# State products of the first eleven heads written to the two score tiles of PSUM, instead of the two rotating tiles

## The chip, the cores and the metric

The kernel runs on one core of one Trainium2 chip. The metric is the device time of one execution in microseconds (us), lower is better; the times shown are medians of several executions. Five engines work side by side: TensorE (PE in the profile; its loads of the stationary operand are listed apart as PEld), VectorE (DVE), ScalarE (ACT), GpSimd (POOL) and SyncE (SP). Matmul results go to PSUM tiles, and DVE and ACT read them there.

## The reference, cut to what matters

One layer of a decoder trunk over 1024 tokens of width 1024. One input projection feeds two mixers, HGRN2 (8 heads, key and value width 128) and GLA (4 heads, key width 128, value width 256). Both are gated linear attention, per head:

```
S_t = diag(a_t) S_{t-1} + k_t v_t^T
o_t = S_t^T (scale * q_t)
```

It can be computed in chunks: with the decays folded into q and k, the output of a chunk is (scores inside the chunk) times v, plus q times the state S left by the chunks before; and each chunk adds its own product k^T v to the state, which is decayed first. Each branch is then normalised, gated and projected, the branches are merged by sigmoid gates, projected again, added to x and normalised.

## The kernel before, in words

Everything is held with channels on the 128 partitions. Large projections are split into a rounded part and a remainder (two fp32r factors, three matmuls for one); they take most of TensorE's time: L607 (`mm_feat`, one 128-channel feature over 1024 tokens, 8 x 6 matmuls of 128x512), L2000 (the value and HGRN stages) and L1422/L1599 (gates, branches, output).

The twelve heads are a side track. `attention` (L639) is a Python generator that is advanced from the main stream of projections (`Stream.weave`): after each unit of projection matmuls the next piece of the running head is issued. Heads run one after the other, the four GLA heads first, then the eight HGRN2 heads; `me` counts them from 1. A tile scheduler then orders the instructions of each engine by priority and by its own costs, and puts in the semaphore waits; so the order on an engine is not quite that of the source. It knows which tile each instruction reads and writes: a write to a tile waits for the earlier readers of the same tile.

A head has 8 chunks of 128 tokens. Its pieces, in order:

- Scores: small matmuls (L665, L698, L756, L762, L767) into the two fixed PSUM tiles `sc_ps[0]` and `sc_ps[1]`. DVE (L676 to L681, L735 to L743, L771) and ACT (L776, L779) read them into `blk` and `scT`.
- Transposes of k (L791) into two tiles from `mtile()`, copied by ACT to `kT` (L792).
- State products (L815): k^T v of chunks 0 to 6 into a PSUM tile `pu`, four chunks to a tile in an HGRN2 head (two tiles), two to a tile in a GLA head (four tiles). DVE takes them into the states one after the other: a copy for the first (L819) and six steps `state(ch+1) = state(ch)*decay + product` (L821). This is called the state chain here. Its seven results are states 1 to 7.
- Outputs: for each half of the chunks one PSUM tile `po` from `mtile()`. For each chunk two matmuls add up there: values times `scT` (L834), and from chunk 1 on state(ch) times q (L836). The state is the stationary operand, so its load on TensorE needs the state. The first output tile needs states 1 to 3, the second states 4 to 7. `post` then reads the tile on ACT (L1177, or L1019 for GLA) and DVE (L1182, L1024).

`mtile()` hands out the two buffers of the pool `ps_m` in turn. In an HGRN2 head these are, in order: two transposes, two state tiles, two output tiles. So the first output tile has the buffer of the first state tile (states 1 to 4), the second that of the second (states 5 to 7).

From head 12's scores on the two score tiles are lent to the projections of the last stages (`scores_done`, L1741).

Of the kernel before, what the change touches and what calls it, by code (L numbers as in the profile page):

```python
# [89 lines left out]
def hybrid_trunk_kernel(  # L90
# [24 lines left out]
    def mtile():  # L115
        cnt[0] += 1
        return ps_m.tile([P, 512], F32, tag="m", name=f"pm{cnt[0]}")

    sc_ps = [ps_s.tile([P, 512], F32, name=f"sc_ps{i}") for i in range(2)]
# [519 lines left out]
    def attention(q, k, f, v, V, post, early, lead=3, next_up=None):  # L639
# [6 lines left out]
        me = head_no[0]  # L646
# [156 lines left out]
        def state(ch):  # L803
            return st[(ch - 1) // spp][:, ((ch - 1) % spp) * V:((ch - 1) % spp + 1) * V]

        def vch(ch):
            n = NCH // len(v)
            return v[ch // n][:, ch % n, :]

        ch = runs = 0  # L810
        while ch < NCH - 1:
            g = min(per, NCH - 1 - ch)
            pu = mtile()
            for i in range(g):
                nc.tensor.matmul(pu[:, i * V:(i + 1) * V], kT[:, ch + i, :], vch(ch + i), start=True, stop=True)  # L815
            for i in range(g):
                u = pu[:, i * V:(i + 1) * V]
                if ch + i == 0:
                    nc.vector.tensor_copy(state(1), u)  # L819
                else:  # L820
                    nc.vector.scalar_tensor_tensor(state(ch + i + 1), state(ch + i), cur[:, ch + i:ch + i + 1], u,  # L821
                                                   ALU.mult, ALU.add)
            ch += g
            runs += 1
            if runs % 2 == 0:
                yield 3
# [171 lines left out]
    def gla_attention(h):  # L998
# [11 lines left out]
        def post(vh, half, po):  # L1010
# [12 lines left out]
            else:  # L1023
                nc.vector.scalar_tensor_tensor(g[vh][:, sl], po, gn, g[vh][:, sl], ALU.mult, ALU.mult)  # L1024

        yield from attention(qk.pop(("q", h)), qk.pop(("k", h)), alphas[h], v, 256, post, early)
        S.free(*v)
        if h < 3:
# [125 lines left out]
    def hgrn_attention(h):  # L1154
# [29 lines left out]
        if ("f", h) not in st:  # L1184
            make_fk(h)
            yield 2
        yield from attention(st.pop(("q", h)), st.pop(("k", h)), st.pop(("f", h)), v, P, post, early,
                             next_up=lambda: h + 1 in stored and load_qf(h + 1))
        S.free(*v)
# [915 lines left out]
```

## Time and profile before

| | |
|---|---|
| median of 3 executions | 1178.21 us (1176.94 to 1178.62) |
| profiled execution | 1176.48 us |
| its span, first to last instruction | 1174.8 us |
| TensorE busy | 1148.9 us, 98% of the span |
| VectorE busy | 842.1 us, 72% |
| ScalarE busy | 646.8 us, 55% |
| granted TensorE clock | 0.998 |

The profile is one execution. In a group or timeline row, the first number is the start, the second the length; "idle before" is how long the engine had stood still, and the arrow names the instruction whose end released it. A matmul's end is modelled, so a row of matmuls overlaps the next one a little; distances are best taken from start to start. A 128x128 fp32 matmul runs in two passes and counts twice: "L834 x4" are two matmuls. A 128x512 matmul of the projections counts once. From 200 to 495 us the span holds the GLA heads and the first HGRN2 scores, from 495 to 820 us the rest of the HGRN2 heads.

### The profile page before, as it was taken

The numbers are of one execution on the slowest core, as the hardware profiler recorded it, in microseconds if no ns is written. First come the engines' busy times: TensorE is split into PE (matmuls) and PEld (weight loads), VectorE is DVE, ScalarE is ACT, GpSimd is POOL, SyncE is SP. The second block draws the span as 40 slices with busy tenths as digits, with TensorE's granted clock in tenths as the row PEclk, the third lists the DMA queues.
The fourth block names the chain that finished last, engine by engine and source line by source line (L and its number), as shares of the span: only waits on it lengthen the run. The fifth ranks groups of instructions, "written<-read, shape, count | busy, mean of one in ns | idle before, by whom it ended". The sixth has DMA issues, their size and how long they took to land.

```text
span 1174.8 us, 20553 instructions
## 1 busy us (share of the span) xinstructions
PE 1148.9 (98%) x8089; PEld 942.3 (80%) x8089; DVE 842.1 (72%) x1316; ACT 646.8 (55%) x963; POOL 138.3 (12%) x285
## 2 busy tenths in 40 slices
PE   7999999999899999999999999999999999999997
PEld 5777888888778888788788888888888888888886
DVE  4755677676686737897697896595543866988994
ACT  5675454284574758646455445566643644534654
POOL 5121111010111101222211110001110000000000
PEclk9999999999999999999999999999999999999999
DMA  9847459486676446988766955156699846435523
GB/s 320 284 151 245 144 193 310 147 281 218 215 247 210 174 142 215 292 279 271 259 205 197 302 164 162 55 172 202 233 321 296 273 155 220 126 109 174 170 95 136
DMA packets 155986, 245.56 MB, mean 209 GB/s; under 512 B 10139, under 2 KB 107473, under 8 KB 155890
## 3 DMA queue, kind: packets, MB, share of 16 engines
q1 hardware_dynamic: 134866, 174.10, 47.3%
q0 software_dynamic: 20976, 70.15, 15.6%
q8 instruction: 63, 1.03, 0.4%
q14 instruction: 33, 0.27, 0.1%
q10 hardware_dynamic: 48, 0.01, 0.0%
HBM read 170.29 MB, written 73.92 MB: 208 GB/s over the span
## 4 chain that ended last, share of the span: by engine, by line
PE 76%; DVE 8%; ACT 7%; DMA 4%; issue 3%; SPq 1%; DVEq 0%; ACTq 0%
PE pd L2000 16%; PE pd L607 15%; PE pd L1422 14%; PE sc_ps L1422 6%; PE pm L1422 6%; PE pd L1599 3%; DMA b<-in_ada_w_dram 2%; PE pd L396 2%; PE pm L834 2%; DMA b<-in_w_in_dram 2%; PE sc_ps L1599 2%; PE pm L836 2%; PE pm L1599 1%; ACT b L211 1%; PE pm L815 1%
## 5 line engine op out<-in xcount | busy, mean ns | idle before, releaser
L607 PE MATMUL pd<-b,b 128*128 128x512 f32 x1248 | 301.2, 395 | 0.0
L607 PEld LDWEIGHTS pd<-b,b 128*128 128x128 f32 x1248 | 230.0, 188 | 48.2
L2000 PE MATMUL pd<-b,b 128*128 128x512 f32 x1008 | 238.4, 393 | 3.8 <-ACT b L211 2.4
L2000 PEld LDWEIGHTS pd<-b,b 128*128 128x128 f32 x1008 | 187.4, 188 | 45.8 <-ACT b L211 2.8
L1422 PE MATMUL pd<-b,b 128*128 128x512 f32 x720 | 169.5, 390 | 0.0
L1422 PEld LDWEIGHTS pd<-b,b 128*128 128x128 f32 x720 | 134.8, 188 | 28.3
L212 DVE TENSOR_TENSOR b<-b,b 128x1024 fp32r<-128x1024 f32 x92 | 110.7, 1221 | 55.0 <-ACT b L211 53.5
L1365 DVE TENSOR_TENSOR b<-b,b 128x1024 fp32r<-128x1024 f32 x56 | 68.1, 1219 | 56.6 <-ACT b L1364 43.3
L211 ACT CAST b<-b 128x1024 fp32r<-128x1024 f32 x92 | 93.6, 1048 | 18.2 <-DMA v<-b 4.3
L1364 ACT CAST b<-b 128x1024 fp32r<-128x1024 f32 x56 | 58.7, 1051 | 68.1 <-PE pm L1422 17.2
L1422 PE MATMUL sc_ps<-b,b 128*128 128x512 f32 x324 | 77.5, 390 | 0.1
L1342 DVE TENSOR_TENSOR b<-b,b 128x1024 fp32r<-128x1024 f32 x48 | 57.8, 1218 | 26.5 <-ACT b L1341 21.7
L1341 ACT CAST b<-b 128x1024 fp32r<-128x1024 f32 x48 | 49.8, 1050 | 39.7 <-PE pd L1422 15.9
L1422 PE MATMUL pm<-b,b 128*128 128x512 f32 x300 | 71.1, 389 | 0.0
L1422 PEld LDWEIGHTS sc_ps<-b,b 128*128 128x128 f32 x324 | 60.6, 188 | 12.9 <-ACT scT L779 0.5
L1422 PEld LDWEIGHTS pm<-b,b 128*128 128x128 f32 x300 | 56.3, 188 | 11.7
L203 DVE TENSOR_TENSOR b<-b,b 128x1024 fp32r<-128x1024 f32 (+1 forms) x37 | 35.7, 977 | 27.5 <-ACT b L202 27.2
L396 PE MATMUL pd<-b,b 128*128 128x512 f32 x192 | 51.8, 403 | 0.9 <-ACT b L202 0.8
L1274 POOL DMA_DIRECT2D ws<-b x64 | 34.6, 540 | 133.3 <-DVE b L1266 48.9
L834 PE MATMUL pm<-scT,b 128*128 128x128 f32 x256 | 47.5, 277 | 2.3 <-DVE b L821 2.0
L726 DVE TENSOR_TENSOR b<-b,tot 128x512 f32<-128x512 f32 x36 | 24.7, 687 | 32.0 <-PE sc_ps L767 30.4
L396 PEld LDWEIGHTS pd<-b,b 128*128 128x128 f32 x192 | 34.3, 188 | 11.9 <-ACT b L202 1.8
(333 smaller groups left out, 1751.9 us busy)
## 6 DMA issues: line engine op xcount, KB each, us to landing
b<-in_w_in_dram SPq DMA_DIRECT2D x64, 512.0 KB, 6.1
ws<-b POOLq DMA_DIRECT2D x64, 256.0 KB, 5.4
b<-ws SPq DMA_DIRECT2D x32, 512.0 KB, 4.1
b<-in_w_in_dram SPq DMA_DIRECT2D x52, 256.0 KB, 4.4
b<-fx SPq DMA_DIRECT2D x24, 512.0 KB, 4.5
b<-in_x_dram SPq DMA_DIRECT2D x16, 512.0 KB, 6.0
b<-in_ada_w_dram SPq DMA_DIRECT2D x32, 256.0 KB, 6.4
v<-b POOLq DMA_DIRECT2D x32, 256.0 KB, 3.5
```

The source lines that it names most:

```text
L211: held(nc.scalar.copy(hi, src))
L212: nc.vector.tensor_sub(lo, src, hi.bitcast(F32))
L396: nc.tensor.matmul(accs[f], wg(a, d, f), b[d][:, half * 512:half * 512 + 512], start=(d == 0 and n == 0), stop=(d == KT - 1 and n == 2))
L607: nc.tensor.matmul(ps[th][0:w, :], a[:, k, 0:w], b[:, th * 512:(th + 1) * 512], start=(k == 0 and n == 0), stop=(k == KT - 1 and n == 2))
L834: nc.tensor.matmul(o, vch(ch)[:, vh * P:(vh + 1) * P], scT[:, ch, :], start=True, stop=(ch == 0))
L1341: nc.scalar.copy(hi, src)
L1342: nc.vector.tensor_sub(lo, src, hi.bitcast(F32))
L1364: nc.scalar.copy(hi, t)
L1365: nc.vector.tensor_sub(lo, t, hi.bitcast(F32))
L1422: nc.tensor.matmul(o, a[:, sl], c, start=(p in (1, 5) and kt == 0 and n == 0), stop=(kt == 3 and n == 2), skip_group_check=True)
L1599: nc.tensor.matmul(o, a, b, start=(p in (1, 5) and kt == 0 and n == 0), stop=(kt == 3 and n == 2), skip_group_check=True)
L2000: nc.tensor.matmul(st.bank[i], l_[:, i * P:(i + 1) * P], r_, start=(p in (1, 5) and kk == 0 and a == 0 and n == 0), stop=(kk == 1 and a == ...
```

## The change

For heads 1 to 11 the state products go to `sc_ps[0]` and `sc_ps[1]` in turn instead of to the next `mtile()`. Head 12 keeps `mtile()`, since the score tiles have been lent by then.

```diff
         ch = runs = 0
         while ch < NCH - 1:
             g = min(per, NCH - 1 - ch)
-            pu = mtile()
+            pu = sc_ps[runs % 2] if me < 12 else mtile()
             for i in range(g):
                 nc.tensor.matmul(pu[:, i * V:(i + 1) * V], kT[:, ch + i, :], vch(ch + i), start=True, stop=True)
```

The buffers of `ps_m` then hold, in an HGRN2 head, only the two transposes and the two output tiles. The first output tile now has the buffer of the first transpose. Every engine has the same number of instructions as before; ACT's and POOL's stand in the same order, SP has two neighbouring loads exchanged, DVE has four small exchanges, and PE differs in six heads (5, 6, 8, 9, 10, 11).

TensorE in head 11 (`pm_7522` is its first output tile, `pm_7533` its second, `b_7465` the states, `b_6854` q; `DVE_49` is DVE's semaphore), before:

```order
L834 MATMUL pm_7522<-scT,b_7328 128x128
L836 MATMUL pm_7522<-b_6854,b_7465 128x128
L607 MATMUL pd_0_7429<-b_146,b_7324 128x512
L607 MATMUL pd_1_7430<-b_146,b_7324 128x512
L607 MATMUL pd_0_7429<-b_154,b_7324 128x512
L834 MATMUL pm_7533<-scT,b_7328 128x128 [waits DVE_49]
L836 MATMUL pm_7533<-b_6854,b_7465 128x128
L834 MATMUL pm_7533<-scT,b_7328 128x128
L836 MATMUL pm_7533<-b_6854,b_7465 128x128
```

and now (`pm_7492` and `pm_7503` are the output tiles, `b_7437` the states, `b_6828` q):

```order
L834 MATMUL pm_7492<-scT,b_7300 128x128
L836 MATMUL pm_7492<-b_6828,b_7437 128x128 [waits DVE_49]
L834 MATMUL pm_7503<-scT,b_7300 128x128 [waits PE_49]
L836 MATMUL pm_7503<-b_6828,b_7437 128x128 [waits DVE_49]
L834 MATMUL pm_7503<-scT,b_7300 128x128
L836 MATMUL pm_7503<-b_6828,b_7437 128x128 [waits DVE_49]
```

The three projection matmuls between the two output tiles have moved behind the second tile. The one wait for DVE at the head of the tile is gone; each L836 now waits for DVE by itself, for the state that it loads. In the other five heads the same happens with 4 (head 5, where one more moves from ahead of the first tile), 2 (6), 4 (8), 4 (9) and 2 (10) projection matmuls.

TensorE at the state products of head 11 (`b_7409` is `kT`, `b_7300` the values), before:

```order
L815 MATMUL pm_7466<-b_7328,b_7437 128x128 [waits DMAHW7_49,Activation_49]
L815 MATMUL pm_7466<-b_7328,b_7437 128x128 x3
L815 MATMUL pm_7475<-b_7328,b_7437 128x128 [waits Activation_49]
L815 MATMUL pm_7475<-b_7328,b_7437 128x128 x2
```

and now:

```order
L815 MATMUL sc_ps_72<-b_7300,b_7409 128x128 [waits DMAHW7_49,Activation_49]
L815 MATMUL sc_ps_72<-b_7300,b_7409 128x128 x3
L815 MATMUL sc_ps_73<-b_7300,b_7409 128x128 [waits DVE_49,Activation_49]
L815 MATMUL sc_ps_73<-b_7300,b_7409 128x128 x2
```

They stand in the same place; the first matmul of the second tile now waits for two engines, for ACT's copy of `kT` as before and for DVE's last read of the score tile.

VectorE behind the state chain of head 11, where its order changes (`pm_7522`, `pm_7533`: the output tiles), before:

```order
L821 SCALAR_TENSOR_TENSOR b_7465<-b_7465,tot_772,pm_7475 128x128
L670 TENSOR_TENSOR b_7420<-b_7420 128x256
L1342 TENSOR_TENSOR b_7772<-b_7680,b_7770 128x1024
L1182 SCALAR_TENSOR_TENSOR b_7116<-pm_7522,vec,b_7116 128x512
L684 TENSOR_TENSOR tot_773<-b_7420 128x256
L1342 TENSOR_TENSOR b_7773<-b_7681,b_7771 128x1024
L1182 SCALAR_TENSOR_TENSOR b_7116<-pm_7533,vec,b_7116 128x512
```

and now:

```order
L821 SCALAR_TENSOR_TENSOR b_7437<-b_7437,tot_772,sc_ps_73 128x128
L670 TENSOR_TENSOR b_7392<-b_7392 128x256
L1342 TENSOR_TENSOR b_7742<-b_7650,b_7740 128x1024
L1182 SCALAR_TENSOR_TENSOR b_7088<-pm_7492,vec,b_7088 128x512
L1182 SCALAR_TENSOR_TENSOR b_7088<-pm_7503,vec,b_7088 128x512
```

The second read of an output tile has moved ahead of two other operations; up to the last step of the state chain (the first row) nothing has moved, here and in the other three places.

## The prediction

> **What bounds the kernel now.** The page's first part, and the waits of TensorE:
>
> ```profile
> PE 1148.9 (98%) x8089; PEld 942.3 (80%) x8089; DVE 842.1 (72%) x1316; ACT 646.8 (55%) x963; POOL 138.3 (12%) x285
> ...
> PE pm L815 <- ACT b L792: 2.0, 6, 0.5
> PE pm L834 <- DVE b L821: 2.0, 5, 0.6
> ```
>
> TensorE is the bound: 1148.9 of 1174.8 us. A change that leaves its work alone can win only its idle time, 25.9 us in all. The two rows under it are the waits at the instructions that the change touches. State products (L815) waiting for ACT's copy of `kT` (L792) need that copy as their operand, whichever PSUM tile they write, so those 2.0 us stay. Output tiles (L834) waiting for the state chain (L821) are another matter: L834 multiplies values by `scT` and needs no state. It waits because its tile is the buffer that the chain still reads. That wait goes.
>
> The timeline of TensorE shows where it is, with the row of projections ahead of each stalled tile; the first two rows are a tile without a stall:
>
> ```profile
> 764.78 4.34 PE L607 MATMUL pd<-b,b 128*128 128x512 f32 x18
> 768.96 0.60 PE L834 MATMUL pm<-scT,b 128*128 128x128 f32 x4
> ...
> 501.60 3.24 PE L607 MATMUL pd<-b,b 128*128 128x512 f32 x13
> 505.11 0.68 PE L834 MATMUL pm<-scT,b 128*128 128x128 f32 x4 [0.27 <-DVE b L821]
> 507.68 0.47 PE L834 MATMUL pm<-scT,b 128*128 128x128 f32 x2
> ...
> 544.65 3.36 PE L607 MATMUL pd<-b,b 128*128 128x512 f32 x14
> 548.18 0.68 PE L834 MATMUL pm<-scT,b 128*128 128x128 f32 x4 [0.17 <-ACT b L1151]
> 549.74 0.71 PE L607 MATMUL pd<-b,b 128*128 128x512 f32 x2
> 550.71 0.49 PE L834 MATMUL pm<-scT,b 128*128 128x128 f32 x2 [0.26 <-DVE b L821]
> ...
> 637.08 1.18 PE L607 MATMUL pd<-b,b 128*128 128x512 f32 x4
> 638.55 0.49 PE L834 MATMUL pm<-scT,b 128*128 128x128 f32 x2 [0.29 <-DVE b L821]
> ...
> 680.95 1.18 PE L607 MATMUL pd<-b,b 128*128 128x512 f32 x4
> 682.27 0.49 PE L834 MATMUL pm<-scT,b 128*128 128x128 f32 x2
> ...
> 726.32 0.71 PE L607 MATMUL pd<-b,b 128*128 128x512 f32 x2
> 727.60 0.49 PE L834 MATMUL pm<-scT,b 128*128 128x128 f32 x2 [0.57 <-DVE b L821]
> ...
> 770.43 0.95 PE L607 MATMUL pd<-b,b 128*128 128x512 f32 x3
> 771.96 0.49 PE L834 MATMUL pm<-scT,b 128*128 128x128 f32 x2 [0.58 <-DVE b L821]
> ```
>
> The first row of each pair is the projections, the second the tile. Without a stall the tile begins 0.16 us before the modelled end of the row ahead (764.78 + 4.34 - 768.96). By that rule the stalls are longer than the brackets say: 505.11 - (501.60 + 3.24 - 0.16) = 0.43 in head 5, 0.33 and 0.42 in head 6, 0.45 in head 8, 0.30 in head 9, 0.73 in head 10, 0.74 in head 11; sum 3.40. The one that the profile puts down to ACT L1151 stands where the first output tile waits for state 4, so I count it with the others. A stall also costs a restart, because the first load is no longer hidden: 0.68 for 0.60 at x4 rows (0.08, twice), 0.47 or 0.49 for 0.39 at x2 rows (0.08 and five times 0.10): 0.74. Removable at most: 4.14 us. The GLA heads and heads 7 and 12 have no such stall; the change gives them nothing.
>
> **The change part by part.** *What is still needed.* Each L836 now waits for its own state. So the question is whether the state is there when its load comes up, in the new order, where the second tile follows the first at once and the projections that stood between come after. Head 7 already runs that way:
>
> ```profile
> 592.29 0.60 PE L834 MATMUL pm<-scT,b 128*128 128x128 f32 x4
> ...
> 593.62 0.39 PE L836 MATMUL pm<-b,b 128*128 128x128 f32 x2
> 593.85 0.39 PE L834 MATMUL pm<-scT,b 128*128 128x128 f32 x2
> ...
> 595.41 0.39 PE L836 MATMUL pm<-b,b 128*128 128x128 f32 x2
> ```
>
> The last L836, the one that loads state 7, starts 3.12 us behind the first L834. The last steps of the chain on DVE, and the first tiles not yet shown:
>
> ```profile
> 507.27 0.33 DVE L821 SCALAR_TENSOR_TENSOR b<-b,tot,pm 128x128 f32<-128x128 f32 x1
> 550.32 0.34 DVE L821 SCALAR_TENSOR_TENSOR b<-b,tot,pm 128x128 f32<-128x128 f32 x1
> 638.13 0.36 DVE L821 SCALAR_TENSOR_TENSOR b<-b,tot,pm 128x128 f32<-128x128 f32 x1
> 681.89 0.32 DVE L821 SCALAR_TENSOR_TENSOR b<-b,tot,pm 128x128 f32<-128x128 f32 x1
> 727.22 0.33 DVE L821 SCALAR_TENSOR_TENSOR b<-b,tot,pm 128x128 f32<-128x128 f32 x1
> 771.58 0.33 DVE L821 SCALAR_TENSOR_TENSOR b<-b,tot,pm 128x128 f32<-128x128 f32 x1
> ...
> 635.60 0.60 PE L834 MATMUL pm<-scT,b 128*128 128x128 f32 x4
> 679.48 0.60 PE L834 MATMUL pm<-scT,b 128*128 128x128 f32 x4
> 724.84 0.60 PE L834 MATMUL pm<-scT,b 128*128 128x128 f32 x4
> ```
>
> State 7 ready against the start of the L836 that uses it: head 6, 550.66 against 547.85 + 3.12 = 550.97; head 8, 638.49 against 638.72; head 9, 682.21 against 682.60; head 10, 727.55 against 727.96; head 11, 771.91 against 772.08. In head 5 the first tile loses its stall and one projection matmul ahead of it (0.23, from 4.18 us for 18): 505.11 - 0.43 - 0.23 = 504.45, plus 3.12 = 507.57 against 507.60. The wait holds the load, about 0.11 us ahead of its matmul (half of the 0.22 from row to row), and a release takes 0.05 (771.91 to 771.96). So head 5 keeps a stall of 507.60 + 0.05 + 0.11 - 507.57 = 0.19; heads 8 and 11 clear it by 0.07 and 0.01, the others by 0.15 and more. The moved projections cost nothing themselves: they run later, behind the tile. DVE's order up to state 7 is unchanged, so these ends hold.
>
> *What the waits cost when they are met.* Seven on L836 in each of seven HGRN2 heads, three in each GLA head: 61. In head 7 the second tile's L834 already carries a wait for DVE that has been met by then; it starts 0.23 us behind the L836 before it (593.62 to 593.85), as between any two. I take nothing. One matmul of each second state tile (heads 5 to 11) now waits for two engines. What an extra wait looks like is in the view of line 834:
>
> ```profile
> L834 PEldq EVENT_SEMAPHORE  x14: 51/51/51, 216.1 to 810.3; - x14
> ```
>
> Seven of 0.051 are 0.36 us if none is hidden, nothing if all are; in head 11 an L834 with such an instruction ahead starts on time (768.96). I take 0.1. The Trainium skill, "Perfetto Trace Analysis", section "Identifying Dependency Chains", says that an instruction that waits for several engines may have such EventSemaphore instructions put before it; the trace agrees (x14), and it changes no term.
>
> *What the score tiles add.* Their readers on ACT (L776, L779) stand ahead of the `kT` copy that L815 waits for anyway, their last reader on DVE (L771) ahead of ACT's copies in program order; and in the new order 36 projection matmuls (8.4 us at 0.23) part a head's output tiles, which need the whole state chain, from the next head's scores. Nothing.
>
> *Where a saved microsecond is lost again.* Head 9:
>
> ```profile
> 672.17 0.81 DVE L1131 TENSOR_SCALAR b<-b,oml,lb 128x1024 f32<-128x1024 f32 x1 [2.50 <-ACT b L1129]
> 699.25 0.42 DVE L694 TENSOR_TENSOR xb<-xb,tot 128x256 f32<-128x256 f32 x1
> ...
> 672.17:699.67 27.50, 26.90 (x196) 22.02 (x194) 27.46 (x47) 12.58 (x20) 3.81 (x8) 1.00 0.60 190
> ...
> 699.82 0.89 PE L698 MATMUL sc_ps<-xb,b 128*32 128x48 f32 x64 [0.39 <-DVE xb L694]
> ...
> 738.16 0.29 DVE L676 TENSOR_TENSOR blk<-sc_ps,eye 128x128 f32<-128x128 f32 x1 [2.34 <-PE sc_ps L665]
> ...
> 780.00:1174.80 394.80, 388.29 (x1958) 321.19 (x1956) 284.11 (x343) 202.86 (x284) 17.19 (x32) 1.00 0.57 190
> ```
>
> From 672.17 to the end of L694 DVE (the third pair in the window row) is busy 27.46 of 27.50 us, and TensorE waits for that end at 699.82. Head 9's tile lies inside, so its 0.30 + 0.10 come back as a longer wait at L698. After head 10 DVE waits 2.34 us for TensorE (738.16): it follows whatever TensorE saves. The chain of waits shows head 9 alone crossing from one head to the next on DVE.
>
> *Sum.* 4.14 - 0.40 (head 9) - 0.19 (head 5) - 0.1 (second waits) - 0.1 (the thin margins of heads 8 and 11) = 3.35, taken as 3.4. From 780 us on TensorE is busy 388.29 of 394.80 us (the last row), so nothing there is likely to take it back. The profiled execution took 1176.48 us (1.68 around its span): it becomes 1173.1. The median shown, 1178.21, lies 1.73 above that execution; from it the forecast is **1174.8 us**. The mechanism's ends: 4.14 with head 9, and 3.76 - 0.30 (head 5) - 0.20 (heads 8, 11) - 0.36 = 2.9; with the 0.7 us to which the three runs shown scatter about their median, 1173.4 to 1176.0.
>
> **The rivals.** *Given back in more places.* If DVE holds TensorE behind heads 10 and 11 as behind head 9, 0.83 + 0.84 go too: 3.4 - 1.7, 1176.5 us. For it: DVE is busy in most of this stretch. Against: the 2.34 us above.
>
> *The wait only changes its place.* If state 7 comes 0.5 us later than before, every last L836 stops for it, and the projections that covered it lie behind. The Trainium skill, "TensorE: Matmul & The Clock Gate", section "HAM oscillation — how this bites in real kernels", tells of a kernel where double-buffering PSUM gave no further gain. By that rule nothing is won here, 1178.2 us. For it: the same L821 is still needed at the end of the tile. Against: it is needed 1.57 us (one tile of 3.12 / 2) later than the buffer was.
>
> *Slower: the waits themselves.* If a wait for DVE at L836, though met, bars the load from running ahead (0.11) and takes an instruction of 0.051, the 61 cost 9.8 us: 1178.2 - 3.4 + 9.8 = 1184.6 us. It cancels the gain from 0.056 us for each wait. Against it is head 7's met wait at no cost; but none of the waits before sat on a load of a fresh state.
>
> **How the numbers follow.** Forecast 0.57, given back 0.29, change of place 0.08, slower 0.06. 0.2% (2.4 us) is about what a measurement of this kernel can tell from no change. Faster: the forecast nearly whole (0.55) and 0.03 of the second, 0.58. Slower 0.06. The same, 0.36. The range takes the mechanism's best end and a little scatter below, and the two cases of no clear change up to no gain: 1173.2 to 1178.1.
>
> **What would show it.** Right: the row of L834 waiting for L821 gone from TensorE's waits, the second output tile 0.22 behind the first one's last L836, with a stall left in head 5 alone, at an L836, of about 0.2 us; L815's wait for L792 still 2.0; L698's wait in head 9 grown from 0.39 to about 0.8; TensorE busy unchanged. Wrong: brackets at L836 in several heads, L836 rows spaced over 0.22, or new waits at L698, L756 or L815. The forecast fails if the chain on DVE ends later than in this profile by more than the margins above.

## The result and the profile after

The changed kernel takes 1173.21 us in the median of 5 runs (1172.94 to 1175.44), the kernel before 1178.26 (5 runs, 1176.94 to 1178.62): ratio 0.9959, 95% interval 0.9947 to 0.9972. It is faster, by 5.05 us in the medians. The profiled executions, on which the prediction's sum was made, differ by less: 1176.48 us before, 1172.94 after, 3.54 us; both had a granted clock of 0.998. The time of one and the same kernel goes with that clock: of 21 executions of the kernel before on one chip, the three at 0.998 took 1176.93 us in the mean, the four at 0.994 1179.42.

TensorE's waits in the profile after, the rows at the lines of the change (the two columns behind the total are how often, and the longest):

```profile
PE 1147.1 (98%) x8089; PEld 942.8 (80%) x8089; DVE 841.5 (72%) x1316; ACT 646.4 (55%) x963; POOL 138.2 (12%) x285
...
PE sc_ps L815 <- ACT b L792: 2.1, 6, 0.5
PE sc_ps L698 <- DVE xb L694: 1.2, 2, 0.8
```

The row of L834 waiting for the state chain (L821), 2.0 us before, is gone. L815's wait for the `kT` copy stands as it did (2.0 before). L698's wait for L694 has grown by 0.4 us: it is head 9's row of the timeline, 0.39 before:

```profile
698.02 0.89 PE L698 MATMUL sc_ps<-xb,b 128*32 128x48 f32 x64 [0.79 <-DVE xb L694]
```

Head 5's output tiles, in the timeline of TensorE after the change:

```profile
504.63 0.60 PE L834 MATMUL pm<-scT,b 128*128 128x128 f32 x4
505.07 0.39 PE L836 MATMUL pm<-b,b 128*128 128x128 f32 x2
...
506.19 0.39 PE L834 MATMUL pm<-scT,b 128*128 128x128 f32 x2
506.41 0.39 PE L836 MATMUL pm<-b,b 128*128 128x128 f32 x2
506.63 0.39 PE L834 MATMUL pm<-scT,b 128*128 128x128 f32 x2
...
507.52 0.39 PE L834 MATMUL pm<-scT,b 128*128 128x128 f32 x2
507.84 0.49 PE L836 MATMUL pm<-b,b 128*128 128x128 f32 x2
```

The second tile's first L834 (506.63) follows 0.22 us behind the L836 ahead of it, as any row does, with no projections between and no stall. Only the last L836, which loads state 7, comes 0.32 behind instead of 0.22, and its 0.49 for 0.39 is the restart. That is the one stall that the prediction left standing. Head 10, whose second tile stood still for 0.73 us before, has no stall left in any row; the end of its first tile, the start of its second and its last row:

```profile
724.85 0.39 PE L836 MATMUL pm<-b,b 128*128 128x128 f32 x2
725.07 0.39 PE L834 MATMUL pm<-scT,b 128*128 128x128 f32 x2
...
726.19 0.39 PE L836 MATMUL pm<-b,b 128*128 128x128 f32 x2
```

How the start of TensorE's work has moved against the kernel before, in us, read from the starts of the rows in the two timelines: at head 5's state products (L815), then at the first L665 of each next head, and, behind head 9, at L698 as well.

| place | before, us | after | won since the row above | forecast |
|---|---|---|---|---|
| head 5, L815 | 500.12 | +0.17 | | |
| behind head 5, L665 | 516.70 | -0.24 | 0.41 | 0.40 |
| behind head 6 | 560.41 | -1.13 | 0.89 | 0.93 |
| behind head 7 | 603.94 | -1.13 | 0 | 0 |
| behind head 8 | 647.81 | -1.73 | 0.60 | 0.55, less a thin margin |
| behind head 9 | 691.55 | -2.19 | 0.46 | 0.40 |
| head 10, L698 | 699.82 | -1.80 | -0.39 | -0.40 |
| behind head 10, L665 | 737.33 | -2.62 | 0.82 | 0.83 |
| behind head 11 | 781.44 | -3.43 | 0.81 | 0.84, less a thin margin |
| last matmul | 1167.99 | -3.54 | 0.11 | 0 |

### The profile page after: what moved, and what is told of

Its sections match the earlier page's. It is cut to its first block, busy times and chain, and to the rows that moved or that the text cites. A ratio compares the mean times of both kernels' runs of the same rounds, so it can differ in the third digit from the quotient of the medians.

```text
span 1171.2 us, 20559 instructions
## 1 busy us (share of the span) xinstructions
PE 1147.1 (98%) x8089; PEld 942.8 (80%) x8089; DVE 841.5 (72%) x1316; ACT 646.4 (55%) x963; POOL 138.2 (12%) x285
## 4 chain that ended last, share of the span: by engine, by line
PE 81%; DVE 7%; ACT 7%; DMA 2%; issue 2%; SPq 1%; ACTq 0%; DVEq 0%
PE pd L607 18%; PE pd L2000 15%; PE pd L1422 14%; PE sc_ps L1422 6%; PE pm L1422 6%; PE pd L396 3%; PE pd L1599 3%; PE pm L834 2%; PE pm L836 2%; PE sc_ps L1599 2%; PE sc_ps L815 2%; PE sc_ps L396 1%; PE pm L1599 1%; ACT b L211 1%; DMA b<-in_ada_w_dram 1%
## 5 line engine op out<-in xcount | busy, mean ns | idle before, releaser
L1422 PE MATMUL pd<-b,b 128*128 128x512 f32 x720 | 169.4, 390 | 0.0
L1422 PEld LDWEIGHTS pd<-b,b 128*128 128x128 f32 x720 | 134.8, 188 | 28.2
L1422 PE MATMUL sc_ps<-b,b 128*128 128x512 f32 x324 | 77.5, 390 | 0.1
L1422 PE MATMUL pm<-b,b 128*128 128x512 f32 x300 | 71.1, 389 | 0.0
L1422 PEld LDWEIGHTS sc_ps<-b,b 128*128 128x128 f32 x324 | 60.6, 188 | 12.9 <-ACT scT L779 0.5
L1422 PEld LDWEIGHTS pm<-b,b 128*128 128x128 f32 x300 | 56.3, 188 | 11.7
L834 PE MATMUL pm<-scT,b 128*128 128x128 f32 x256 | 46.8, 275 | 0.0
```

What stands on the lines that cost most here:

```text
L834: nc.tensor.matmul(o, vch(ch)[:, vh * P:(vh + 1) * P], scT[:, ch, :], start=True, stop=(ch == 0))
L1422: nc.tensor.matmul(o, a[:, sl], c, start=(p in (1, 5) and kt == 0 and n == 0), stop=(kt == 3 and n == 2), skip_group_check=True)
```

## The experiments

In every text below, "head by head" is the shift of the table above, taken between that kernel's trace and the trace before.

### Which heads carry it: HGRN2 alone, GLA alone

```diff
-            pu = mtile()
+            pu = sc_ps[runs % 2] if 4 < me < 12 else mtile()   # HGRN2 heads 5 to 11
```
```diff
-            pu = mtile()
+            pu = sc_ps[runs % 2] if me < 5 else mtile()        # GLA heads
```

> Only heads 5 to 11 (HGRN2) write their state products to the score tiles; the four GLA heads keep the rotating tiles. Theory of the shared buffer: the GLA heads never stalled at an output tile, so this is the whole change: in the trace TensorE is 3.5 us earlier than before from head 11 on (0.41 after head 5, 1.3 after head 6, 1.9 after head 8, 2.8 after head 10, 3.6 after head 11), and the time is that of the change, 4 to 5 us under the kernel before. Rival, that the GLA heads carry the 1.4 us by which the medians of the change and of before differ more than their two traces: the time then is only some 3.5 us under before.

> Only heads 1 to 4 (GLA) write their state products to the score tiles. The order of every engine is that of before; only the tiles and with them the waits differ. Theory of the shared buffer: no stall there, no gain: within 0.5 us of before, head by head the same starts. Rival, GLA heads carry 1.4 us: 1.4 us under before. Rival, met waits cost: three more waits on L836 in each GLA head, 12 in all, 0.16 us each, 1.9 us above before.

HGRN2 alone took 1174.80 us (5 runs) against 1179.33 (19 runs of the kernel before on that chip), ratio 0.9959, interval 0.9946 to 0.9973: all of the change's ratio. Head by head its trace repeats the change's: -0.43, -1.32, -1.91, -2.34, back to -1.99, -2.85, -3.66. GLA alone took 1178.34 us (10 runs), ratio 0.9993, interval 0.9982 to 1.0004, no difference; from head 5's L815 to head 12's its shift stays between +2.56 and +2.75 (1.3 us of that were lost ahead of 109 us and 1.5 between 308 and 333 us, where no changed line stands; other kernels' traces lose it there too, the one of the kernel before without its bias add, below, 1.5 us). Its waits at the output tiles are those of before:

```profile
PE pm L834 <- DVE b L821: 2.2, 6, 0.6
```

So nothing is won or lost in the GLA heads, although 12 of the 61 new waits stand there. With the change the shift over heads 1 to 4 is constant too, +0.16 at head 1's L665 and +0.17 at head 5's.

### The other side of the sharing: the outputs moved, the state products left

```diff
-                po = mtile()
+                po = sc_ps[half] if 4 < me < 12 else mtile()
```

> The other way round: in heads 5 to 11 the output tiles go to the two score tiles, and the state products keep the rotating tiles. Theory of the shared buffer: what counts is that states and outputs no longer share, not which of them moves; the stalls at L834 go as in the change, 3.5 us in the trace, since the next head's scores come 36 projection matmuls after the outputs, by when ACT and DVE have read them. Rival, that the score tiles suit the states only: the next head's first scores (L665) wait for the readers of the outputs, a stall of up to 1 us in each of six heads, and the gain is 0 or less.

1175.35 us (5 runs) against 1179.33, ratio 0.9963, interval 0.9950 to 0.9977. From head 5's L815 to head 12's its shift goes from +2.95 to -0.56, 3.51 us won, against the change's 3.65, in nearly the same portions (0.41, 0.89, 0.60, 0.46, 0.42 lost, 0.71, 0.80 at the places of the table; the 0.71 stands for 0.82 because 0.15 more is lost between L698 and head 10's L815, which was not followed up). TensorE's waits again have no row of L834. Which of the two gets the score tiles makes no difference: it is their parting that wins. That also answers what the change did to the score tiles' readers: two ways of using them, one result.

The order of TensorE's matmuls is the same in this kernel, in HGRN2 alone and in the change: in all three the projections stand behind the second tile. The new order can't win by itself, since with a shared buffer a second tile that comes up earlier would wait the longer for the same step of the chain. What it adds to the parting, or costs, is not shown: no kernel here parts the tiles and keeps the old order.

### The change again

> The changed kernel itself, timed beside the other three. If the two traces tell all, its median is 3.5 us under before's; if before's profiled execution was merely a fast one of its kind, 4.5 to 5 us, as measured the first time.

1174.61 us (6 runs), 4.7 us under the 1179.33 of before in the medians; ratio 0.9962, interval 0.9948 to 0.9977. Its trace has the table's shifts to within 0.1 us up to head 12 (-3.48 at L665), but at the last matmul it is only 2.19 us ahead: 1.2 us are lost at 874.81, in a place that is looked at below.

### Head 9 alone, and heads 10 and 11 alone

```diff
+            pu = sc_ps[runs % 2] if me == 9 else mtile()
```
```diff
+            pu = sc_ps[runs % 2] if 9 < me < 12 else mtile()
```

> Head 9 alone writes its state products to the score tiles. Theory, given back at L698: TensorE is 0.4 us earlier than before from head 9's second output tile to the next head's L665 (starts at 691.55 before), and back level (within 0.05) at that head's L698 (699.82 before), whose wait for DVE L694 grows from 0.39 to about 0.8. Rival, that the 0.4 is kept: 0.4 us earlier to the end.

> Heads 10 and 11 alone write their state products to the score tiles. Theory: each keeps its 0.83, so TensorE is level until head 10's second output tile, 0.83 us earlier after it and 1.67 earlier after head 11, to the end. Rival, given back behind these heads as behind head 9: 0 to 0.8.

With head 9 alone the shift goes from +0.85 at its L815 to +0.42 behind it (0.43 won) and to +0.77 at head 10's L698 (0.35 returned), where TensorE waits for VectorE, 0.39 before:

```profile
700.59 0.59 PE L698 MATMUL sc_ps<-xb,b 128*32 128x48 f32 x37 [0.75 <-DVE xb L694]
```

At the end it is +0.75: of 0.43 us 0.08 are left at L698, and 0.10 at the end. With heads 10 and 11 alone the shift goes from +0.81 to -0.04 behind head 10 and to -0.85 behind head 11, and stays there to the last matmul (-0.87): 1.66 us, all kept. The times, one execution of each, can't tell such amounts (1177.26 and 1175.63 us, 1178.52 for the kernel before); the traces carry this. They decide between the forecast and the first rival: what is won is given back behind head 9 and nowhere else.

### Less work for VectorE behind head 9

The gate-bias add (L1104, 1.20 us on VectorE between head 9's chain and L694) is left out, with the change and without it. Both kernels thus leave the gate bias out of the computation.

```diff
-        nc.vector.tensor_add(gacc[0:1, :], gacc[0:1, :], gbias[0:1, :])
+        pass
```

> The changed kernel without one DVE operation, the addition of the gate's bias (L1104, 1.2 us, inside the stretch in which DVE is busy without a gap between head 9 and the next head's L698; the gate's bias is left out of what is computed). Theory, DVE holds TensorE there: the wait at L698 (0.8 us with its restart 0.9) goes, and TensorE is 0.8 to 0.9 us earlier than in the changed kernel from there to the end, so head 9's 0.4 is kept after all. Rival, that L698 waits for something else: no difference.

> The kernel before without the same DVE operation (the gate's bias left out). Theory: only the wait at L698 that was there goes, 0.4 to 0.5 us earlier than before from L698 to the end. The difference between this and the run with the change is then the whole gain of seven stalled tiles, 3.9 to 4.0 us, instead of the 3.5 between the change and before. Rival: 3.5, as between those.

Both expectations missed. One execution of each took 1177.21 us with the change and 1177.66 without it. The scheduler did not only drop the add: it put L698 four projection matmuls (0.91 us) earlier on TensorE. So in the changed kernel the wait stayed, 0.69 us for 0.79, although L694 ended 0.99 us earlier relative to head 9's L815; without the change it was gone:

```profile
699.42 0.89 PE L698 MATMUL sc_ps<-xb,b 128*32 128x48 f32 x64 [0.69 <-DVE xb L694]
```

```profile
700.30 0.89 PE L698 MATMUL sc_ps<-xb,b 128*32 128x48 f32 x64
```

(The first row is the kernel with the change, the second the one without it.) From head 9's L815 to head 11's L665 the change wins 0.47 us between these two kernels, 0.89 between the originals; from head 5's L815 to head 12's it wins 3.22 and 3.65. That VectorE sets L698 is seen again. That the 0.4 us come back when VectorE has room is not shown, because the order of TensorE changed with it.

### A chain that ends later

In heads 5 to 11 one more VectorE copy stands ahead of each of the last three steps of the state chain; its target is written again before it is read.

```diff
                 u = pu[:, i * V:(i + 1) * V]
+                if 4 < me < 12 and ch + i > 3:
+                    nc.vector.tensor_copy(blk.rearrange("p c t -> p (c t)")[:, 0:P], u)
```

> The change with one VectorE copy of 128x128 more (into a block that is written again before it is read) ahead of each of the last three steps of the state chain, in heads 5 to 11. Theory (the change wins because the last state is ready before the last L836 wants it, by margins of 0.01 to 0.4 us): state 7 comes three copies later, 0.6 to 0.8 us in all, which is more than every margin, so L836 now stops in heads 5, 6, 8, 10 and 11 (and 7 or 9 perhaps), about 0.4 to 0.8 us each with a restart of 0.1, and by the start of head 12's L815 it is 2.5 to 4 us behind the change, near or behind the kernel before. Rival (once the output has a tile of its own the chain's end no longer matters): no waits at L836, the same start at head 12 as the change, within 0.3 us. Head 9's extra VectorE time also goes to L698 under both, up to 0.7 us.

The rival's number came out (-1.33 at head 12's L815 after +2.59 at head 5's: 3.92 us won, against 3.65 with the change; one execution, 1175.71 us), but not for the rival's reason: the chain ended earlier, not later. Head 5's last steps of the chain on VectorE, with the added copies (L817), the TensorE rows behind them:

```profile
507.21 0.35 DVE L821 SCALAR_TENSOR_TENSOR b<-b,tot,sc_ps 128x128 f32<-128x128 f32 x1
507.47 0.29 DVE L817 COPY blk<-sc_ps 128x128 f32<-128x128 f32 x1
507.67 0.35 DVE L821 SCALAR_TENSOR_TENSOR b<-b,tot,sc_ps 128x128 f32<-128x128 f32 x1
507.93 0.29 DVE L817 COPY blk<-sc_ps 128x128 f32<-128x128 f32 x1
508.13 0.35 DVE L821 SCALAR_TENSOR_TENSOR b<-b,tot,sc_ps 128x128 f32<-128x128 f32 x1
...
509.94 0.39 PE L834 MATMUL pm<-scT,b 128*128 128x128 f32 x2
510.17 0.39 PE L836 MATMUL pm<-b,b 128*128 128x128 f32 x2
```

Copies of 0.29 us took the places of the gate's larger operations (L1150, 0.69; L658, 0.64; L659, 0.86) that stand between these steps otherwise, and those went behind. State 7 is ready 5.76 us after the start of L815 instead of 7.49, so the last L836 (510.17) no longer stalls: head 5 now gives 0.60 us, the change's 0.41 and the 0.19 that the prediction had taken off. Heads 6, 8, 9, 10 and 11 give 0.91, 0.58, 0.40, 0.85 and 0.81, as with the change, though their state 7 too is ready 1.2 to 2.0 us earlier. So beyond being in time the chain has nothing more to give. Behind head 9, 0.31 us are lost again by head 10's L815 (0.43 with the change), with 0.87 us of waiting at L698, which the profile puts down to ScalarE's L202. As L698 stands four projection matmuls earlier on TensorE here too, this doesn't show what the copies cost there. What a late chain costs was not tried here; a kernel of the next section shows it by accident.

### The remaining wait at L815: the kT copy first

The wait that the prediction left alone, L815 for ACT's copy of `kT`, is taken away by setting that copy ahead of the gate's activations, with the change and without it.

```diff
-            nc.scalar.copy(kT[:, g * 4:g * 4 + nt, :].rearrange("p c s -> p (c s)"), pt[:, 0:nt * P])
+            with tc.high_priority(offset=EVICT_FIRST):
+                nc.scalar.copy(kT[:, g * 4:g * 4 + nt, :].rearrange("p c s -> p (c s)"), pt[:, 0:nt * P])
```

> The change with ScalarE's copy of kT (L792) set ahead of the gate's activations (L1129) that stood before it, in every head. Theory (L815's wait for L792, 2.0 us over the heads, was untouched by the change and is a separate stall): the row of L815 waiting for L792 goes, 0.4 to 0.7 us with a restart of 0.1 each in heads 7, 8, 10 and 11, while L1129 and with it L1131 on VectorE start about 1 us later, so that head 9's L698 wait grows by up to 1 us. Net against the change 1 to 2.4 us less, 1170.8 to 1172.2 on the scale on which the change takes 1173.2; against the kernel before about 5 to 6 us in the trace. Rival (VectorE takes the place: everything that L815 saves is waited for at L698 in more heads): the same time as the change within 0.5 us, with L698 waits of over 1 us in two heads or more.

> The kernel before with the same move of ScalarE's kT copy. Theory (the two stalls are apart, one behind the other on TensorE): L815's wait goes, but since L815 then starts and ends earlier than before by the same amount as the output tile, the chain on VectorE ends earlier too and L834 still waits for L821 about as long (2.0 us in the brackets, 0.3 to 0.7 a head); 1 to 2.4 us less than the kernel before, and the change's own gain on top of it (against the run of the change with the same move) is again about 3.5 us. Rival (one and the same delay seen at two places): with L815 early the chain is early, L834 stops no more, and this kernel gains 4 us or more alone while the change adds under 1.

Waits of the kernel before with the copy first, and one of its stalled tiles, head 10's:

```profile
PE pm L834 <- DVE b L821: 3.0, 6, 0.9
PE pm L815 <- ACT b L792: 0.4, 1, 0.4
...
727.03 0.49 PE L834 MATMUL pm<-scT,b 128*128 128x128 f32 x2 [0.92 <-DVE b L821]
```

L815's wait shrinks from 2.0 to 0.4 us, and L834's grows from 2.0 to 3.0: products that come earlier wait longer for a chain whose VectorE work has not become less. From head 5's L815 to head 12's this kernel wins 1.53 us, in the expected range; measured, 1176.95 us (10 runs) against 1178.45 (21 runs), ratio 0.9987, interval 0.9977 to 0.9998. With the change it wins 5.95 us over the same stretch, 2.30 more than the change alone and 4.42 more than the copy alone. So the two stalls are apart, and the rival (one delay seen twice, the change then adding under 1) is out; the change's portion is larger than 3.65, and than the 3.5 expected, as L834's waits, which it takes away, had grown instead of staying at 2.0.

The change with the copy first also shows a late state on L836. In head 9, where VectorE has no idle time, TensorE reaches the tile earlier than state 6 is ready (679.76, the end of its step on VectorE); the L836 ahead of it has already stood for 0.14 us:

```profile
678.79 0.49 PE L836 MATMUL pm<-b,b 128*128 128x128 f32 x2
679.11 0.39 PE L834 MATMUL pm<-scT,b 128*128 128x128 f32 x2
679.82 0.49 PE L836 MATMUL pm<-b,b 128*128 128x128 f32 x2 [0.32 <-DVE b L821]
```

The last two rows stand 0.71 us apart where 0.22 is usual. The stall of the output tile is back, at an L836, as the prediction's second rival had it, but in this one head. L698's wait behind head 9 has not grown, as the theory (by up to 1 us) and the rival (over 1 us in two heads or more) had it: it is 0.37 us, put down to ScalarE's L202, with L698 three matmuls earlier on TensorE.

Over all, though, little of the 2.3 us can be seen: 1172.65 us (5 runs), above the 1170.8 to 1172.2 expected; ratio 0.9956, interval 0.9943 to 0.9969, beside 0.9959 and 0.9962 for the change. Intervals of this width, 1.5 us to each side, neither show nor exclude it. At the last matmul its trace is 3.85 us ahead of before, 5.62 at head 12. Of the 1.77 us lost between, 1.60 lie at one place, TensorE's L1422 (rows of four kernels, in each ScalarE's cast and TensorE's matmul that needs it: before, after, the change again, the change with the copy first):

```profile
875.38 1.05 ACT L1364 CAST b<-b 128x1024 fp32r<-128x1024 f32 x1 [5.15 <-DMA b<-ws]
...
877.15 2.22 PE L1422 MATMUL pd<-b,b 128*128 128x512 f32 x9
```

```profile
871.78 1.05 ACT L1364 CAST b<-b 128x1024 fp32r<-128x1024 f32 x1 [4.68 <-DMA b<-ws]
...
873.64 5.60 PE L1422 MATMUL pd<-b,b 128*128 128x512 f32 x24
```

```profile
873.22 1.05 ACT L1364 CAST b<-b 128x1024 fp32r<-128x1024 f32 x1 [5.41 <-DMA b<-ws]
...
874.81 1.45 PE L1422 MATMUL pd<-b,b 128*128 128x512 f32 x5 [1.02 <-ACT pd L1405]
```

```profile
871.61 1.04 ACT L1364 CAST b<-b 128x1024 fp32r<-128x1024 f32 x1 [6.79 <-DMA b<-ws]
...
873.20 5.73 PE L1422 MATMUL pd<-b,b 128*128 128x512 f32 x24 [1.44 <-ACT pd L1405]
```

The cast waits for a load of `ws` (512 KB). Where TensorE stands still, it starts 1.59 us behind the cast (874.81 - 873.22, 873.20 - 871.61). Before the distance was 1.77 and after 1.86, so both had 0.2 to 0.3 us to spare: the load is just in time. In the change's second trace it landed 1.2 us too late, and with the copy first 1.60. Of the fourteen traces, the four in which TensorE came to this matmul latest (877.15 to 879.82 us, the kernel before among them) show no stall; of the ten others, which came at 871.60 to 876.78, seven do, of 0.38 to 1.97 us. The DMA engines are full ahead of it, in the profile after (the last numbers are the granted clock, the DMA share and GB/s):

```profile
850.00:870.00 20.00, 20.00 (x89) 16.55 (x89) 7.40 (x7) 7.82 (x11) 5.37 (x10) 1.00 1.01 337
```

That a kernel that comes earlier meets this load more often fits these fourteen; that this is its cause was not tried.

### The gate-bias add on GpSimd

On top of the change with the copy first, the add L1104, which holds L694 behind head 9, goes from VectorE to GpSimd.

```diff
-        nc.vector.tensor_add(gacc[0:1, :], gacc[0:1, :], gbias[0:1, :])
+        nc.gpsimd.tensor_add(gacc[0:1, :], gacc[0:1, :], gbias[0:1, :])
```

> The change with the kT copy moved as in the run before, and the gate-bias add (L1104) on GpSimd in place of VectorE. Theory (between head 9's L1131 and L694 VectorE has no idle time and holds TensorE at L698): about 1 us less work on VectorE ahead of L694 wherever the add lies in that stretch, L698's wait in head 9 gone or under 0.3 us, 0.4 to 1 us less than the run with the kT move alone. Rival (the add is late on GpSimd, or its order on the engines changes more than its cost): L698 or a later activation waits for GpSimd instead, the same or slower by up to 1 us.

1175.95 us (11 runs), ratio 0.9975, interval 0.9966 to 0.9984: 3.3 us more than without this move, of which the stretch from head 5's L815 to head 12's has 2.2 (3.76 us won for 5.95); the rest is not explained. That is worse than either theory, and the rows of GpSimd, VectorE and TensorE say why:

```profile
690.12 4.71 POOL L1104 TENSOR_TENSOR b<-b,b 1x1024 f32<-1x1024 f32 x1 [0.50 <-DVE b L1101]
...
692.66 2.66 DVE L670 TENSOR_TENSOR b<-b 128x256 f32<-128x256 f32 x1
...
700.65 0.89 PE L698 MATMUL sc_ps<-xb,b 128*32 128x48 f32 x64 [2.47 <-DVE xb L694]
```

The add takes 4.71 us on GpSimd for 1.20 on VectorE, and VectorE's L670, 0.62 us in the median of its twelve, takes 2.66 beside it and ends 0.5 us after the add. TensorE then waits 2.47 us at L698, for 0.37 without the move (put down to ScalarE's L202 there, so it is not sure that the add held L698 in that kernel).

## Why the prediction was right, and where it was not

**What bounds.** Matmuls and their number are the same; TensorE's busy time, which the prediction held unchanged, fell by 1.8 us (1148.9 to 1147.1), its idle time by as much. The prediction's own rule for a stall says why both did: 0.16 us of each lie under the modelled end of the row ahead (seven, 1.1 us) and the restarts (0.74, less the 0.10 that stays in head 5) are counted as busy.

**The sum, term by term.** The seven stalls and their restarts went, at the places named, each within 0.06 us of its term (the table). Taken off for head 9 were 0.40, measured 0.39 and, with head 9 alone, 0.35. Taken off for head 5 were 0.19; the kernel with the earlier chain gave 0.60 in head 5 instead of 0.41, the 0.19. Two terms were too careful: 0.1 for the second waits and 0.1 for thin margins. Nothing of the first was seen: the start of TensorE's work moves by 0 in head 7, which has seven new waits at L836 and one at its second state tile. And heads 8 and 11 gave 0.60 and 0.81, without a margin 0.55 and 0.84. 3.35 forecast, 3.65 by head 12's L815, 3.54 in the profiled pair. (In the lower end, 3.76 should read 3.74, 4.14 less 0.40; 2.9 stays.)

**L815's wait for the kT copy stays.** Right: 2.0 and 2.1 us. The chip showed moreover that it is a stall of its own.

**The median.** Here one step failed: "The median shown, 1178.21, lies 1.73 above that execution; from it the forecast is 1174.8". The offset was carried over to the changed kernel as if it were a constant, but the changed kernel's profiled execution lies only 0.27 under its median. Both profiled executions had a clock of 0.998, and a median mixes clocks: the changed kernel's five ran at 0.995 to 0.998, those of the first executions before are not on record. The forecast for the profiled execution, 1173.1, was measured as 1172.94, by the mechanism forecast. The median, 1173.21, came out 1.6 lower than its forecast and 0.01 above the low end of the range; that it fell inside is luck. Its gain, 5.05 us, is more than the 4.14 that the prediction held removable at most. When the change was timed again, its median was 1174.61. The two ratios, 0.9959 and 0.9962, are 4.8 and 4.5 us, with intervals that begin at 3.3 and 2.7, so 3.5 lies inside both. At equal clocks (0.994, 0.995, 0.996 and 0.997), on the chip of that second timing, the change is faster by 3.2, 4.4, 3.6 and 3.3 us, in means of one to seven executions. Whether anything beyond 3.5 is more than scatter between executions stays open. Nothing at the changed lines explains it.

**The rivals.** *Given back in more places*: heads 10 and 11 alone kept 1.66 of 1.66 us. *The wait only changes its place*: not in this kernel, except for head 5's 0.19 us; but with the kT copy first it did in head 9 (0.71 us for 0.22): state 6, which is in time by 0.55 us in the change, came 0.9 us later behind L815, and the tile 0.5 us earlier. The case of another kernel that the prediction weighed against the change, from the Trainium skill, "TensorE: Matmul & The Clock Gate", section "HAM oscillation — how this bites in real kernels", did not carry over: separate PSUM tiles gave 3.5 us here, by either way of parting them. *Slower*: 0.056 us for each met wait was its point of decision; the twelve over heads 1 to 4 moved the start of TensorE's work by 0.01 us together, the seven in head 7 by nothing.

## What to carry to other kernels

A PSUM buffer that rotates between a producer that reads late and a consumer that needs nothing of it makes a wait that no data asks for: look for a matmul whose listed releaser does not write its operands. What such a stall is worth is its length by start-to-start distances plus its restart, less what the next engine without idle time takes back, and both can be read head by head from one trace. Before counting on a second gain behind the first, look along the later program for a load that is only just in time.

## What the runs showed of the hardware that was not expected

- A wait that is met costs TensorE nothing here: an L836 with a met wait for VectorE starts 0.22 us behind its L834, as in head 5 above (506.19 and 506.41), and an L834 as much behind its L836 (506.41 and 506.63).
- GpSimd took 4.71 us for an add of 1x1024 that VectorE does in 1.20, and a VectorE multiplication of two SBUF operands beside it took 2.66 us for 0.62. The Trainium skill, "SBUF — State Buffer", section "Who interferes with whom", says that a VectorE instruction with two SBUF inputs contends with a GpSimd instruction that reads SBUF; the row of L670 agrees. Two VectorE multiplications just ahead, inside the span that the profile gives to the add (L668, 0.96 us, L669, 0.63), were not held up.
- One more instruction ahead of a step of a chain on VectorE made that chain end 1.7 us earlier in head 5, because in the scheduler's order it took the place of longer ones.
